# Other pads in SBUF: activations begin, modulo 256 bytes, where the weights begin that they are multiplied with

## The chip, the core and the metric

The kernel is one program on one core of a Trainium2 chip. Its metric is the device time of one execution in microseconds (us). The engines named below are PE (TensorE, matmul), PEld (TensorE's weight loads), DVE (VectorE), ACT (ScalarE), POOL (GpSimd) and SP (SyncE, which issues the DMAs of the weights). SBUF is the on-chip memory from which PE reads both operands of a matmul; a tile's "begin" is its byte address within a partition.

## The reference: what is computed

A trunk of two layers over 256 tokens of width 2048, all in float32. Layer 0 mixes tokens with a Conformer convolution module, layer 1 with multi-head latent attention; each is followed by a squared-ReLU MLP of width 8192. Before every part stands an RMSNorm, after it a residual add, and at the end one more RMSNorm.

```
x = x + conv_module(rms_norm(x), pw1 2048x4096, depthwise width 31, LayerNorm, swish, pw2 2048x2048)
x = x + square(relu(rms_norm(x) @ w1)) @ w2            # w1 2048x8192, w2 8192x2048
x = x + mla(rms_norm(x), w_in 2048x1088, w_q_up 512x3072, w_kv_up 512x4096, w_o 2048x2048)
x = x + square(relu(rms_norm(x) @ w1)) @ w2
out = rms_norm(x)
```

Nearly all arithmetic is in the products with these weights, 364 MB that are read from HBM once.

## The kernel before: stages, tiles and their names

**Products in two parts.** Every float32 operand is written as a high part and a low part in the matmul type float32r (hi, lo for weights; xt, sh and sl, kvh and kvl, qh and ql, oh and ol for activations), and a product is three matmuls: high by high, high by low, low by high. A weight tile comes by DMA into raw; ACT copies it into hi, and DVE (in the convolution also POOL) subtracts to make lo. The profile writes a matmul as `acc<-a,b`: a is the operand that is streamed through the array (256, 288 or 512 columns), b the one that is loaded into it beforehand (128 columns, a PEld row). A weight load runs beside the matmul before it.

**Which operand is streamed.** Three forms matter:

- `mm3` (lines 194 to 196) streams the weights and loads the activations. It carries the second pointwise product of the convolution (pw2, activations sh and sl_, 512 columns), both MLPs' second product (activations sh, sl, gh, gl), the attention's input product (w_in, activations xt, first 288 columns at a time, then 512), its value projections (activations kvh, kvl, 256 columns) and its output product (w_o, activations oh, ol, 512 columns).
- lines 844 to 846 (pw1 of the convolution) stream the activations xt, 256 columns, and load hi and lo. Lines 1408 to 1410 and 1431 to 1433 (keys and queries) do the same with kvh, kvl, qh, ql.
- lines 505 and 506 (both MLPs' first product) load a block of hi and stream 512 columns of xt, high and low part side by side, and then load the block of lo and stream the 256 columns of the high part:

```python
for j in range(8):
    k = 8 * h + j
    nc.tensor.matmul(ps[0], wh[:, j, :], xhl(k), start=k == 0, stop=False)
    nc.tensor.matmul(ps[0][:, :S], wl[:, j, :], xh(k), start=False, stop=k == KC - 1)
```

So one unit of w1, 16 blocks of 128 rows, is 16 pairs of a 512-column and a 256-column matmul. There are 128 such units in the two MLPs, 2048 pairs.

**The order of the work** is written out by hand: inside `tc.manual_schedule()` the instructions of each engine stand in the order of the code. In an MLP, `ORDERS` interleaves the units of w1 (T) with those of w2 that use seven products in place of eight (S) and plain ones (O), so that a unit of 505 and 506 stands between runs of 21 or 24 matmuls of lines 194 to 196. The first 16 units of each MLP follow each other without such runs.

**Where tiles begin.** Tiles are placed by pools, one after the other, each begin a multiple of 32 bytes. Five small tiles that nothing reads are there for the place alone: `pad_const`, `pad_small`, `pad_right` (below xt, and below the attention's keys, values and queries, on the right side of SBUF), `pad_kv` and `pad_o` (in the attention's pool `at`). All of hi, lo and raw begin at 64 modulo 256, in every stage. The blocks that one matmul takes of a tile begin a multiple of 256 bytes further on, except in the first part of w_in (288 columns), where the second half of hi and lo begins 128 further on.

Of the kernel before, what the change touches and what calls it, by code (L numbers as in the profile page):

```python
# [10 lines left out]
F32 = mybir.dt.float32  # L11
# [7 lines left out]
P = 128  # L19
# [16 lines left out]
PARTS = 4  # L36
PAD_CONST = 24
PAD_SMALL = 32
PAD_RIGHT = 48
PAD_KV = 8  # L40
PAD_O = 56
WB = 6
LOOK = WB // 2 - 1
LAST_PE = 22
# [37 lines left out]
def trunk_kernel(  # L82
# [26 lines left out]
    nc = tc.nc  # L109
# [22 lines left out]
    edge = ctx.enter_context(tc.tile_pool(name="edge", bufs=1, side="right"))  # L132
    pad_right = edge.tile([P, PAD_RIGHT], F32, name="pad_right")
    nc.gpsimd.memset(pad_right, 0.0)
# [655 lines left out]
    with ExitStack() as cx:  # L790
        cv = cx.enter_context(tc.tile_pool(name="cv", bufs=1, reuse_waits="tile"))
# [12 lines left out]
        b2 = cv.tile([P, D], F32, name="b2")  # L804

        cn = cv.tile([P, T, D], F32, tag="tok", name="cn")
        sh = cv.tile([P, KC, S], F32R, name="sh")
        sl_ = cv.tile([P, KC, S], F32R, name="sl_")
        stats = cv.tile([P, T, KC // 2, 6], F32, name="stats")

        UC = 2
# [429 lines left out]
    with ExitStack() as cx:  # L1241
        at = cx.enter_context(tc.tile_pool(name="at", bufs=1, reuse_waits="tile"))
# [92 lines left out]
                if h == 1:  # L1335
                    u_load(u + 3)

        pad_kv = at.tile([P, PAD_KV], F32, name="pad_kv")
        nc.gpsimd.memset(pad_kv, 0.0)
        kvh = at.tile([P, KR // P, S], F32R, name="kvh")  # L1340
        kvl = at.tile([P, KR // P, S], F32R, name="kvl")
        qh = at.tile([P, QR // P, S], F32R, name="qh")
# [15 lines left out]
        for i in range(2):  # L1358
            for j in range(HG):
                nc.scalar.activation(qpB[i][DR:, j, :], mq[DR:, :], AF.Copy)  # L1360
        pad_o = at.tile([P, PAD_O], F32, name="pad_o")
        nc.gpsimd.memset(pad_o, 0.0)
# [413 lines left out]
```

## Time and profile before

| | |
|---|---|
| time, median of 3 runs | 1942.49 us (1942.22 to 1942.64) |
| time of the profiled execution | 1942.55 us |
| its span, first to last instruction | 1940.8 us |
| PE busy in the span | 1915.5 us (99%), 10778 matmuls |
| DVE busy | 1652.4 us (85%) |
| ACT busy | 1208.8 us (62%) |
| DMA | 367.62 MB, mean 189 GB/s |
| granted TensorE clock, mean | 0.998 |

PE's rows in the timeline give a start and a length. Matmuls overlap, since the next is started while the last still drains, so a row's length (0.39 us for 512 columns) is more than what the matmul costs. What it costs is the distance from its start to the next one's. Over a run without a stall, first and last start divided by the number of matmuls between them give that price to a fraction of a nanosecond, though single starts are given to 10 ns.

### The profile page before, as it was taken

How to read it: one execution, taken by the hardware profiler on the slowest of the kernel's cores; microseconds unless marked ns; L12 is line 12 of the kernel's file. 1: busy time of each engine (PE TensorE's matmuls, PEld its weight loads, DVE VectorE, ACT ScalarE, POOL GpSimd, SP SyncE). 2: the span in 40 equal slices, each digit the busy share in tenths (PEclk: the TensorE clock that was granted, in tenths of full speed). 3: DMA queues.
4: the chain of work that ended last, by engine and by line, in shares of the span. 5: the costliest groups of instructions: out<-in, count | busy, mean ns of one | idle time of the engine just before them, and what ended most of it. 6: DMA issues, size and time to landing. Idle time of an engine off the chain costs nothing.

```text
span 1940.8 us, 28480 instructions
## 1 busy us (share of the span) xinstructions
PE 1915.5 (99%) x10778; PEld 1673.4 (86%) x10778; DVE 1652.4 (85%) x2372; ACT 1208.8 (62%) x1709; POOL 223.9 (12%) x184
## 2 busy tenths in 40 slices
PE   7999999999999999999999999999999999999998
PEld 7999888888888888888899998888888888888886
DVE  5999865789999999999976665657999999999887
ACT  5556654766666666666566665566766666666654
POOL 5999400000000000000001410000000000000000
PEclk9999999999999999999999999999999999999999
DMA  8666355857666667666646445765667666766663
GB/s 236 184 177 191 133 196 153 227 171 209 200 199 207 197 201 211 197 200 211 202 144 180 118 150 174 206 183 168 200 191 210 208 195 195 214 200 196 210 222 109
DMA packets 407113, 367.62 MB, mean 189 GB/s; under 512 B 15416, under 2 KB 351936, under 8 KB 406720
## 3 DMA queue, kind: packets, MB, share of 16 engines
q1 hardware_dynamic: 405952, 363.63, 62.6%
q10 hardware_dynamic: 1024, 2.17, 0.3%
q8 instruction: 84, 1.38, 0.3%
q14 instruction: 53, 0.43, 0.1%
HBM read 363.68 MB, written 2.10 MB: 188 GB/s over the span
## 4 chain that ended last, share of the span: by engine, by line
PE 95%; DVE 2%; ACT 1%; DMA 1%; POOL 1%; issue 0%; DVEq 0%; ACTq 0%; POOLq 0%
PE acc L505 24%; PE acc L194 15%; PE acc L196 15%; PE acc L195 15%; PE acc L506 12%; PE acc L846 3%; PE acc L845 3%; PE acc L844 3%; PE acc L250 1%; PE sum L894 1%; PE acc L1544 0%; POOL lo L169 0%; DMA xs<-in_x 0%; ACT hi L168 0%; PE acc L1408 0%
## 5 line engine op out<-in xcount | busy, mean ns | idle before, releaser
L505 PE MATMUL acc<-xt,hi 128*128 128x512 f32 x2048 | 716.6, 393 | 0.0
L420 DVE TENSOR_TENSOR lo<-raw,hi 128x1024 fp32r<-128x1024 f32 (+1 forms) x512 | 570.8, 1121 | 92.5 <-ACT hi L419 92.2
L506 PE MATMUL acc<-xt,lo 128*128 128x256 f32 x2048 | 574.2, 280 | 0.5 <-DVE lo L420 0.5
L419 ACT ACTIVATE hi<-raw 128x1024 fp32r<-128x1024 f32 (+1 forms) x512 | 480.3, 971 | 73.2 <-PE acc L195 67.2
L505 PEld LDWEIGHTS acc<-xt,hi 128*128 128x128 f32 x2048 | 384.4, 188 | 87.2
L506 PEld LDWEIGHTS acc<-xt,lo 128*128 128x128 f32 x2048 | 385.2, 188 | 4.1 <-DVE lo L420 0.8
L194 PE MATMUL acc<-hi,sh 128*128 128x512 f32 x930 | 364.3, 392 | 0.0
L196 PE MATMUL acc<-lo,sh 128*128 128x512 f32 x930 | 362.9, 390 | 0.0
L195 PE MATMUL acc<-hi,sl 128*128 128x512 f32 x802 | 312.3, 389 | 0.0
L168 ACT ACTIVATE hi<-raw 128x1024 fp32r<-128x1024 f32 (+2 forms) x184 | 180.0, 1005 | 47.0 <-PE acc L195 41.7
L196 PEld LDWEIGHTS acc<-lo,sh 128*128 128x128 f32 x930 | 174.6, 188 | 37.9
L194 PEld LDWEIGHTS acc<-hi,sh 128*128 128x128 f32 x930 | 174.6, 188 | 36.9
L169 DVE TENSOR_TENSOR lo<-raw,hi 128x1024 fp32r<-128x1024 f32 (+2 forms) x118 | 133.2, 1148 | 68.8 <-ACT hi L168 63.0
L419 ACT ACTIVATE hi<-V 128x1024 fp32r<-128x1024 f32 x94 | 99.6, 1059 | 129.2 <-DVE V L712 118.4
L195 PEld LDWEIGHTS acc<-hi,sl 128*128 128x128 f32 x802 | 150.7, 188 | 28.9
L946 DVE SCALAR_TENSOR_TENSOR sum<-ub,w_dw,sum 128x256 f32<-128x256 f32 x400 | 162.8, 480 | 7.6 <-ACT sum L902 6.5
L169 POOL TENSOR_TENSOR lo<-raw,hi 128x1024 fp32r<-128x1024 f32 x66 | 157.6, 2410 | 24.0 <-ACT hi L168 24.0
L419 ACT ACTIVATE hi<-T 128x1024 fp32r<-128x1024 f32 x94 | 99.4, 1057 | 89.3 <-DVE T L700 80.2
L511 ACT ACTIVATE U<-acc 128x512 f32<-128x512 f32 x128 | 76.2, 595 | 112.5 <-PE acc L506 112.0
L844 PE MATMUL acc<-xt,hi 128*128 128x256 f32 x512 | 145.3, 284 | 0.0
L845 PE MATMUL acc<-xt,hi 128*128 128x256 f32 x512 | 143.9, 281 | 1.0 <-DVE xt L207 1.0
L846 PE MATMUL acc<-xt,lo 128*128 128x256 f32 x512 | 144.0, 281 | 0.1
(270 smaller groups left out, 2797.3 us busy)
## 6 DMA issues: line engine op xcount, KB each, us to landing
raw<-in_mlp_w SPq DMA_DIRECT2D x256, 1024.0 KB, 6.2
raw<-in_conv_w_pw SPq DMA_DIRECT2D x64, 512.0 KB, 5.5
raw<-in_conv_w_pw SPq DMA_DIRECT2D x16, 1024.0 KB, 5.1
raw<-in_mla_w_o SPq DMA_DIRECT2D x16, 1024.0 KB, 5.6
raw<-in_mla_w_kv_up SPq DMA_DIRECT2D x8, 1024.0 KB, 5.5
raw<-in_mla_w_in SPq DMA_DIRECT2D x8, 576.0 KB, 3.8
raw<-in_mla_w_in SPq DMA_DIRECT2D x4, 1024.0 KB, 6.6
raw<-in_mla_w_q_up SPq DMA_DIRECT2D x16, 256.0 KB, 4.6
```

The source lines that it names most:

```text
L168: nc.scalar.activation(hi, raw[:, js, :], AF.Copy)
L169: eng.tensor_tensor(lo, raw[:, js, :], hi.bitcast(F32), op=ALU.subtract)
L194: nc.tensor.matmul(ps, sh, mh, start=start, stop=False)
L195: nc.tensor.matmul(ps, sl, mh, start=False, stop=False)
L196: nc.tensor.matmul(ps, sh, ml, start=False, stop=stop)
L419: nc.scalar.activation(parts[0], src, AF.Copy)
L420: nc.vector.tensor_tensor(parts[1], src, parts[0].bitcast(F32), op=ALU.subtract)
L505: nc.tensor.matmul(ps[0], wh[:, j, :], xhl(k), start=k == 0, stop=False)
L506: nc.tensor.matmul(ps[0][:, :S], wl[:, j, :], xh(k), start=False, stop=k == KC - 1)
L844: nc.tensor.matmul(o, wh[:, bs], xh(k), start=k == 0, stop=False)
L845: nc.tensor.matmul(o, wh[:, bs], xl(k), start=False, stop=False)
L846: nc.tensor.matmul(o, wl[:, bs], xh(k), start=False, stop=k == KC - 1)
```

## The change

Only places change. `pad_right` shrinks from 48 to 40 floats, `pad_kv` goes, `pad_o` grows from 56 to 64 floats, and two new pads stand in the convolution's pool ahead of sh and behind sl_. PE, ACT, DVE and SP run the same instructions in the same order as before, with the same waits; POOL has one instruction less, the memset of `pad_kv`.

```diff
-PAD_RIGHT = 48
-PAD_KV = 8
-PAD_O = 56
+PAD_RIGHT = 40
+PAD_SH = 16
+PAD_STATS = 48
+PAD_O = 64
...
         cn = cv.tile([P, T, D], F32, tag="tok", name="cn")
+        cv.tile([P, PAD_SH], F32, name="pad_sh")
         sh = cv.tile([P, KC, S], F32R, name="sh")
         sl_ = cv.tile([P, KC, S], F32R, name="sl_")
+        cv.tile([P, PAD_STATS], F32, name="pad_stats")
         stats = cv.tile([P, T, KC // 2, 6], F32, name="stats")
...
-        pad_kv = at.tile([P, PAD_KV], F32, name="pad_kv")
-        nc.gpsimd.memset(pad_kv, 0.0)
         kvh = at.tile([P, KR // P, S], F32R, name="kvh")
```

The begins that follow from it, modulo 256 bytes, as the built programs have them:

| tiles | used by | before | after |
|---|---|---|---|
| hi, lo (weights) | all | 64 | 64 |
| xt (turned tokens) | pw1, w1 of both MLPs, w_in | 32 | 64 |
| sh, sl_ (gated rows of the convolution) | pw2 | 0 | 64 |
| kvh, kvl, qh, ql | key, value and query projections | 96 | 64 |
| kpA, kpB, qpB (rotary parts, mask) | scores | 96 | 64 |
| kTh, kTl, qTh, qTl, qpA, vv, pT | scores, values | 32 | 64 |
| sh, sl, gh, gl (hidden rows of the MLPs) | second product of both MLPs | 64 | 64 |
| oh, ol | w_o | 64 | 64 |

Everything else keeps its begin modulo 256 bytes.

## The prediction

> **What bounds the kernel now.** I read the page first: busy time, clock and the chain that ended last.
>
> ```profile
> span 1940.8 us, 28480 instructions
> PE 1915.5 (99%) x10778; PEld 1673.4 (86%) x10778; DVE 1652.4 (85%) x2372; ACT 1208.8 (62%) x1709; POOL 223.9 (12%) x184
> PEclk9999999999999999999999999999999999999999
> PE 95%; DVE 2%; ACT 1%; DMA 1%; POOL 1%; issue 0%; DVEq 0%; ACTq 0%; POOLq 0%
> ```
>
> PE is busy throughout, holds 95% of the chain, and its clock is granted in full. So the time is the sum of what 10778 matmuls cost from start to start, and whatever changes that price changes the time. The page's groups give the counts; their mean ns is a matmul's length and not its price.
>
> ```profile
> L505 PE MATMUL acc<-xt,hi 128*128 128x512 f32 x2048 | 716.6, 393 | 0.0
> L506 PE MATMUL acc<-xt,lo 128*128 128x256 f32 x2048 | 574.2, 280 | 0.5 <-DVE lo L420 0.5
> L844 PE MATMUL acc<-xt,hi 128*128 128x256 f32 x512 | 145.3, 284 | 0.0
> ```
>
> The prices come from PE's timeline: first and last start of a run without a stall, one row each, divided by the matmuls between them. First 512 columns: w_o, then pw2, then the second part of w_in.
>
> ```profile
> 1218.84 0.39 PE L194 MATMUL acc<-hi,oh 128*128 128x512 f32 x1
> ...
> 1237.20 0.39 PE L194 MATMUL acc<-hi,oh 128*128 128x512 f32 x1
> ```
> ```profile
> 280.83 0.39 PE L194 MATMUL acc<-hi,sh 128*128 128x512 f32 x1
> ...
> 298.69 0.39 PE L194 MATMUL acc<-hi,sh 128*128 128x512 f32 x1
> ```
> ```profile
> 1022.59 0.39 PE L194 MATMUL acc<-hi,xt 128*128 128x512 f32 x1
> ...
> 1027.48 0.40 PE L194 MATMUL acc<-hi,xt 128*128 128x512 f32 x1
> ```
>
> The same line, shape and clock, and three prices: 18.36 us for 81 matmuls is 226.7 ns, 17.86 us for 78 is 229.0 ns, 4.89 us for 21 is 232.9 ns. By the table of begins, weights and activations both begin at 64 in w_o; in pw2 the activations begin at 0, in w_in at 32. So the distance of the begins does seem to cost, and 512 columns are cheapest at equal begins. Now 256 columns: pw1 (xt at 32 streamed, weights at 64 loaded), then keys (kvh at 96 streamed), then values (kvh at 96 loaded).
>
> ```profile
> 76.39 0.28 PE L844 MATMUL acc<-xt,hi 128*128 128x256 f32 x1
> ...
> 86.33 0.28 PE L844 MATMUL acc<-xt,hi 128*128 128x256 f32 x1
> ```
> ```profile
> 1045.59 0.28 PE L1408 MATMUL acc<-kvh,hi 128*128 128x256 f32 x1
> ...
> 1048.39 0.28 PE L194 MATMUL acc<-hi,kvh 128*128 128x256 f32 x1
> ...
> 1051.23 0.28 PE L1408 MATMUL acc<-kvh,hi 128*128 128x256 f32 x1
> ```
>
> 9.94 us for 84 is 118.3 ns, 2.80 us for 24 is 116.7 ns, 2.84 us for 24 is 118.3 ns. pw1 and values have one thing in common: the loaded operand begins 32 bytes behind the streamed one. So it is the distance between the two that counts, not either place. Last the pairs of lines 505 and 506, two runs of them:
>
> ```profile
> 348.43 0.39 PE L505 MATMUL acc<-xt,hi 128*128 128x512 f32 x1
> ...
> 392.81 0.39 PE L505 MATMUL acc<-xt,hi 128*128 128x512 f32 x1
> ```
> ```profile
> 1267.62 0.39 PE L505 MATMUL acc<-xt,hi 128*128 128x512 f32 x1
> ...
> 1335.45 0.39 PE L505 MATMUL acc<-xt,hi 128*128 128x512 f32 x1
> ```
>
> 44.38 us for 128 pairs is 346.7 ns; 67.83 us for 192 pairs is 353.3 ns. The instructions and the distance of the begins are the same. So a pair has two rhythms; starting up differently, it stays in one or the other. In the trace 17 of the 128 units run in the dear one (the first two of layer 0's MLP, the first fifteen of layer 1's), 111 in the cheap one. The mean pair is (111 x 346.7 + 17 x 353.3) / 128 = 347.6 ns.
>
> **The change part by part.** No instruction moves on PE, so each term is a count times a difference in price.
>
> *pw2* (384 matmuls, 128 of each line) goes from distance 64 to equal begins: 229.0 to 226.7, -0.9 us. *w_in, second part* (96 matmuls): 232.9 to 226.7, -0.6 us. *w_in, first part* (192 of 288 columns) has half its blocks 128 apart after the change, for which no row stands; I take -0.3 us, between 0 and -0.6 (half of the 6.2 ns that the 512 columns gain, 192 times).
>
> *w_o and the MLPs' second product* are at equal begins already, 0. But they show what equal begins do when the width has just changed. This is a run of w2 behind a unit of w1:
>
> ```profile
> 711.71 0.40 PE L194 MATMUL acc<-hi,sh 128*128 128x512 f32 x1
> ...
> 713.33 0.39 PE L195 MATMUL acc<-hi,sl 128*128 128x512 f32 x1
> 713.56 0.39 PE L196 MATMUL acc<-lo,sh 128*128 128x512 f32 x1
> ...
> 716.28 0.39 PE L196 MATMUL acc<-lo,sh 128*128 128x512 f32 x1
> ```
>
> The first seven take 1.62 us, 231.4 ns each; the last twelve 2.72 us, 226.7 ns. So the 226.7 is not the price of equal begins as such. It is that of a rhythm into which several equal matmuls in a row settle.
>
> *256 columns at equal begins* stand in the scores alone, four in a row behind a stall:
>
> ```profile
> 1080.15 0.27 PE L195 MATMUL acc<-kTh,qTl 128*128 128x256 f32 x1
> ...
> 1080.62 0.28 PE L194 MATMUL acc<-hi,kvh 128*128 128x256 f32 x1
> ```
>
> 0.47 us for four is 117.5 ns, between 116.7 and 118.3. So *pw1* (1536) could gain 1536 x 1.6 ns = 2.5 us if it settles, or lose some 2 us if not; I take 0. *Keys and queries* (384 at 116.7 now) lose at most 0.6 us, *values and the rotary queries* (288 at 118.3) gain at most 0.5; together 0. The scores' own operands move together, 0.
>
> *The pairs* are the large term: 2048 of them, 712 us, and every nanosecond is 2.0 us. No row shows a pair at equal begins. From below: 226.7 for the 512 columns and 116.7 for the 256, 343.4 ns, -8.6 us. From above: the dear rhythm in all units, 353.3 ns, +11.7 us. Between them: the width changes at every matmul of a pair, so the settled 226.7, which took seven of a kind, is not reached; 231.4 and an unsettled 118.3 make 349.7 ns, +4.3 us. What speaks for the upper half is that the same pairs, in a wrong rhythm, do cost 353.3. I take the middle of these two, 351.5 ns: 3.9 x 2048 = +8.0 us.
>
> One rule of the Trainium skill speaks against any effect. TensorE: Matmul & The Clock Gate, section "Step-by-step: what each phase is for", has two independent SBUF read ports on PE, one for the streamed operand and one for the weight load, so that loading the next block takes no bandwidth from the running matmul; by that, pads change nothing. The trace doesn't agree: 226.7, 229.0 and 232.9 ns stand for one instruction.
>
> *The memset of pad_kv*: one on POOL of 105 ns, for which nobody waits.
>
> ```profile
> L1339 POOL MEMSET pad_kv<- x1: 105/105/105, 896.6 to 896.6; 128x8 f32 x1
> ```
>
> Its cover is POOL's idle time (busy 223.9 of 1940.8 us); bare it would be 0.1 us. DVE and ACT read and write the moved tiles 32 or 64 bytes further on, 0 within their slack (85% and 62% busy); if a gain in PE's pace met the wait for DVE's lo, little would be lost, for that wait is 0.5 us in all 2048 of line 506.
>
> *Sum*: 8.0 - 0.9 - 0.6 - 0.3 = +6.2 us on a span of 1940.8; with the 1.75 us around it (1942.55 less 1940.8) that is 1948.8, and the profiled execution is within 0.1 us of the median 1942.49. I forecast 1949, slower.
>
> **The rivals.** *Equal begins suit the pairs too.* Then 512 columns run at 226.7 within a pair and 256 at 116.7: pairs -8.6, pw1 -2.5, pw2 and w_in -1.8, in all -12.9 us, 1929.6. If only the 17 dear units mend, the pairs gain 2048 x 0.9 = 1.8, and with pw1 and the rest it is -6.1, 1936.4; 1933 is the middle. For it: at 512 columns equal is the cheapest of three distances, and a common distance in w1 and w2 might spare the seven dear matmuls at each change. Against it: the cheap rhythm of 346.7 is within 3.3 ns of the two cheapest rows taken together (343.4), so 111 of the 128 units have little left to win and much to lose. It decides if the pair falls under 346 ns.
>
> *Nothing moves beyond the small terms*: pairs and pw1 keep their prices by another rhythm, -1.8 us, 1941; the skill's two ports come to the same, 1942.5 by that rule. Against it: five prices for two shapes in one trace.
>
> *The pads don't do what they say*: excluded as far as places go, the built program has them; only the relation to cost is open.
>
> **How the numbers follow.** Slower by the pairs 0.52, faster by the pairs 0.35, nothing beyond the small terms 0.13. What a measurement here tells from no change is about 0.2%, 3.9 us. The slower case alone reaches from 1945 (+4.3 less 1.8) to 1953 (+11.7 less 1.8), and 1956 if pw1 loses too; the faster one from 1930 to 1937. A tenth at either end left out, the range is 1931 to 1956. Some of the slower case falls inside 0.2%, as does the third: faster 0.35, same 0.14, slower 0.51.
>
> **What would show it.** In the profile after: L505 to L505 at 350 ns or more in most units (right), or under 346 (wrong, the first rival). pw2 and w_in at 226.7 from start to start. pw1 within 116.7 and 119.5. w2's first seven matmuls behind a unit of w1 are where a common rhythm would show. Order, waits and idle time of PE should be as before; a new wait in front of PE would mean that I have the wrong mechanism altogether.

## The result, and the profile after

The changed kernel takes 1951.29 us, median of 4 runs (1950.55 to 1952.12), against 1942.36 us for the kernel before (4 runs, 1942.12 to 1942.64): a ratio of 1.0046, with a 95% interval of 1.0029 to 1.0063. It is slower, by 0.5%. The forecast was 1949. Two runs further down, one of 4960 us of the kernel before and one of 3211 us of the kernel under "All but xt", lie far outside all others of their kernels and are left out of the ratios.

The page of the kernel after, the same rows as were shown of before (the lines of the code stand one to three further down, so 505 is now 506):

```profile
span 1949.9 us, 28480 instructions
PE 1925.8 (99%) x10778; PEld 1679.9 (86%) x10778; DVE 1653.8 (85%) x2372; ACT 1208.9 (62%) x1709; POOL 223.8 (11%) x183
PEclk9999999999999999999999999999999999999999
PE 97%; DVE 1%; ACT 1%; DMA 1%; issue 0%; SPq 0%; DVEq 0%; ACTq 0%
L506 PE MATMUL acc<-xt,hi 128*128 128x512 f32 x2048 | 725.0, 397 | 0.0
L507 PE MATMUL acc<-xt,lo 128*128 128x256 f32 x2048 | 574.9, 281 | 0.6 <-DVE lo L421 0.6
```

POOL has one instruction less, the memset of `pad_kv`; the clock is granted in full, DVE and ACT have what they had, and the wait for lo is 0.6 us in all. PE's busy time grew by 10.3 us, and 8.4 of that is one group: line 506, whose mean length went from 393 to 397 ns. Its 256-column partner, line 507, gained 0.7. PE waits for nothing new; the same matmuls cost more.

Now the prices from PE's timeline. Two stretches of pairs, the first from layer 0, the second from layer 1:

```profile
355.22 0.40 PE L506 MATMUL acc<-xt,hi 128*128 128x512 f32 x1
...
406.10 0.40 PE L506 MATMUL acc<-xt,hi 128*128 128x512 f32 x1
```
```profile
1285.06 0.39 PE L506 MATMUL acc<-xt,hi 128*128 128x512 f32 x1
...
1340.52 0.39 PE L506 MATMUL acc<-xt,hi 128*128 128x512 f32 x1
```

50.88 us for 144 pairs is 353.3 ns; 55.46 us for 160 pairs is 346.6 ns. These are the two means that the kernel before had, at the same two places, exchanged: before, layer 0's stretch was the cheap one and layer 1's the dear one. Over the trace 109 of the 128 units run dear once settled and 17 cheap: the second and third unit of layer 0's MLP, the second to sixteenth of layer 1's. Before, just these 17 were the dear ones and 109 the cheap. (The prediction took the first two and the first fifteen for the dear ones and all others for cheap. The first unit of each MLP, which is entered from the transposes of xt, is in neither count here; its later pairs were dear before, 353.3 and 352.3 ns, and are cheap after.)

The cheap rhythm is the same pair again and again. The dear one is not, and it has another form after the change: before, pairs of 345.7 and 360.9 ns took turns; after, two pairs of 349.6 in the mean are followed by one of 360.8. Both come to 353.3. The expectations further down give the dear price as 353.5 or 353.6 and mean the same rhythm.

Then the smaller terms: pw1, keys, pw2 and the second part of w_in.

```profile
76.74 0.28 PE L847 MATMUL acc<-xt,hi 128*128 128x256 f32 x1
...
86.46 0.28 PE L847 MATMUL acc<-xt,hi 128*128 128x256 f32 x1
```
```profile
1057.32 0.28 PE L1409 MATMUL acc<-kvh,hi 128*128 128x256 f32 x1
...
1060.08 0.28 PE L1411 MATMUL acc<-kvh,lo 128*128 128x256 f32 x1
```
```profile
281.31 0.39 PE L195 MATMUL acc<-hi,sh 128*128 128x512 f32 x1
...
298.99 0.39 PE L195 MATMUL acc<-hi,sh 128*128 128x512 f32 x1
```
```profile
1029.01 0.39 PE L195 MATMUL acc<-hi,xt 128*128 128x512 f32 x1
...
1033.79 0.39 PE L195 MATMUL acc<-hi,xt 128*128 128x512 f32 x1
```

pw1: 9.72 us for 81 matmuls, 120.0 ns where it was 118.3. Keys: 2.76 us for 23, 120.0 where it was 116.7. So 256 columns at equal begins cost 120 ns, the dearest of the three. pw2: 17.68 us for 78, 226.7 where it was 229.0. w_in: 4.78 us for 21, 227.6 where it was 232.9. So 512 columns at equal begins, one after the other, are the cheapest.

Last, a run of w2 behind a unit of w1:

```profile
432.60 0.40 PE L195 MATMUL acc<-hi,sh 128*128 128x512 f32 x1
...
433.99 0.39 PE L195 MATMUL acc<-hi,sh 128*128 128x512 f32 x1
...
437.16 0.39 PE L197 MATMUL acc<-lo,sh 128*128 128x512 f32 x1
```

The first six cost 231.7 ns each (1.39 us), the other fourteen 226.4 (3.17 us). In the mean of the 74 such runs the first six cost 230.8 ns, where they cost 231.8 before. It still has to settle at each handover, though xt now begins where sh and the weights begin.

The ledger, made from all the starts of both timelines (each matmul's start to the next one's, with the stalls in it):

| part | before to after, us |
|---|---|
| the pairs of w1 (mean 348.4 to 352.4 ns; 347.8 to 351.8 without the five pairs that hold a stall) | +8.2 |
| pw1 | +1.5 |
| keys and queries | +0.5 |
| values and the rotary part of the queries | +0.4 |
| transposes, stalls included | +0.6 |
| w2 of both MLPs | -0.9 |
| pw2 | -0.6 |
| w_in, both parts | -0.6 |
| sum, and the span's change | +9.1 |

From here on a mean pair leaves out the five that hold a stall, and a mean of pw1 the 21 or 22 of its 1536 matmuls that do.

### The profile page after: what moved, and what is told of

Its sections match the earlier page's. It is cut to its first block, busy times and chain, and to the rows that moved or that the text cites. A ratio compares the mean times of both kernels' runs of the same rounds, so it can differ in the third digit from the quotient of the medians.

```text
span 1949.9 us, 28480 instructions
## 1 busy us (share of the span) xinstructions
PE 1925.8 (99%) x10778; PEld 1679.9 (86%) x10778; DVE 1653.8 (85%) x2372; ACT 1208.9 (62%) x1709; POOL 223.8 (11%) x183
## 4 chain that ended last, share of the span: by engine, by line
PE 97%; DVE 1%; ACT 1%; DMA 1%; issue 0%; SPq 0%; DVEq 0%; ACTq 0%
PE acc L506 24%; PE acc L195 15%; PE acc L196 15%; PE acc L197 15%; PE acc L507 12%; PE acc L848 3%; PE acc L847 3%; PE acc L849 3%; PE acc L251 1%; PE sum L897 1%; DMA xs<-in_x 0%; PE acc L1432 0%; PE acc L1433 0%; PE acc L1434 0%; PE acc L1409 0%; PE acc L1410 0%
## 5 line engine op out<-in xcount | busy, mean ns | idle before, releaser
L506 PE MATMUL acc<-xt,hi 128*128 128x512 f32 x2048 | 725.0, 397 | 0.0
```

## Experiments

The theory to test: the price of a matmul depends on how far apart, modulo 256 bytes, its two operands begin, the pairs of w1 carry the change, and equal begins are bad for them because the width changes at every matmul. The rivals: the place in SBUF itself counts and not the distance; the small parts carry it; the rhythm is set only by how a unit is entered.

**Only xt moves.** The kernel before with one pad changed.

```diff
-PAD_RIGHT = 48
+PAD_RIGHT = 40
```

> Only xt (and the attention's keys, queries and values) move from 32 to 64; the gated rows, the latents and the rotary parts stay as before. If the pairs of lines 505 and 506 carry the change, this alone gives 1942.4 + 8.2 (pairs) + 1.5 (pw1) - 0.6 (w_in) = 1951.5 us, and pairs cost 353.6 ns in some 110 of 128 units. If the loss came from the other moved tiles, it stays at 1942 to 1944.

Measured: 1951.8 us (4 runs, 1950.23 to 1953.28) against 1940.87 for the kernel before on the same chip, a ratio of 1.0054 (1.0039 to 1.0069). From its page, and a unit of pairs between two runs of w2 from PE's timeline:

```profile
span 1948.4 us, 28480 instructions
L505 PE MATMUL acc<-xt,hi 128*128 128x512 f32 x2048 | 723.9, 397 | 0.0
```
```profile
710.53 0.39 PE L505 MATMUL acc<-xt,hi 128*128 128x512 f32 x1
...
715.82 0.40 PE L505 MATMUL acc<-xt,hi 128*128 128x512 f32 x1
```

15 pairs in 5.29 us, 352.7 ns. Here 98 units are dear and 28 cheap, the mean pair is 351.3 ns, and pw1 is at 120.0. One pad smaller by 32 bytes makes the whole loss, within the interval.

**All but xt.** The changed kernel with that pad put back.

```diff
-PAD_RIGHT = 40
+PAD_RIGHT = 48
```

> The whole change without the move of xt: gated rows and latents at 64, xt at 32. By the matmuls' prices: pw2 -0.5 us, keys, queries and values +0.9 us, pairs 0: 1942.8 us, within 0.1% of before, with pairs at 346.7 ns in 111 units. If moving the rest matters on its own, it is more than 2 us away from before.

Measured: 1942.49 us (median of 10 runs), a ratio of 1.0006 (0.9996 to 1.0016): not to be told from no change.

```profile
L506 PE MATMUL acc<-xt,hi 128*128 128x512 f32 x2048 | 716.0, 393 | 0.0
```
```profile
706.75 0.40 PE L506 MATMUL acc<-xt,hi 128*128 128x512 f32 x1
...
711.95 0.39 PE L506 MATMUL acc<-xt,hi 128*128 128x512 f32 x1
```

15 pairs in 5.20 us, 346.7 ns, 113 units cheap and 13 dear. The 13 are not among those that were dear in the kernel before: here the fourth to sixteenth unit of layer 0's MLP are dear, and all of layer 1's are cheap, though xt and the weights begin where they did. By the same ledger pw2 gained 0.6 us, keys and queries lost 0.5 and values 0.4: the small parts nearly cancel. The two ratios together, 1.0060, agree with the 1.0046 of the whole change within their intervals.

**The weights move, not xt.** The kernel before, xt where it was (32), and all tiles of the weights' side of SBUF moved to 32 modulo 256.

```diff
-PAD_CONST = 24
+PAD_CONST = 16
```

> The other way round: xt stays at 32, and the weights with everything on the left side of SBUF move from 64 to 32, so that xt and weights begin together without xt being moved. If the distance of the two begins sets the price, the pairs cost 353.6 ns in most units, pw1 120 ns, and the time is 1951 us as after the change. If it is xt's place at 64 as such, the pairs stay at 346.7 and the time at 1942.

Measured in one run: 1951.82 us.

```profile
span 1950.0 us, 28480 instructions
```
```profile
712.10 0.39 PE L505 MATMUL acc<-xt,hi 128*128 128x512 f32 x1
...
717.39 0.40 PE L505 MATMUL acc<-xt,hi 128*128 128x512 f32 x1
```

352.7 ns a pair, 111 units dear, pw1 at 120.0: the changed kernel's prices, with xt where the faster kernel has it. For equal begins it is the distance between the two that counts and not either place.

**Another way into a unit.** The changed kernel with a 128-column transpose ahead of each unit of w1. It adds 128 matmuls of its own.

```diff
                             ps.append(acc_tile())
+                            nc.tensor.transpose(ps[0][:, :P], ident, ident)
```

> The changed kernel with one 128-column transpose more ahead of each of the 128 units of w1 (its result is overwritten). It adds some 128 x 110 to 170 ns = 14 to 22 us of its own. If the rhythm of a unit is set by how it is entered, the transpose ends the hand-over from w2's run, and the units behind w2 no longer stand at 353.6: all 128 units come out in one rhythm, most likely 346.7 ns a pair. If equal begins as such make the pairs dear, the units behind w2 stay at 353.6 and only the first fifteen of layer 1 are at 346.7.

Measured in one run: 1965.6 us. The 14.3 us over the changed kernel are the transposes and what they hold up, 112 ns for each of the 128. A unit from PE's timeline, with its transpose:

```profile
714.85 0.27 PE L503 MATMUL acc<-ident 128*128 128x128 f32 x1
714.88 0.48 PE L507 MATMUL acc<-xt,hi 128*128 128x512 f32 x1
...
715.32 0.40 PE L507 MATMUL acc<-xt,hi 128*128 128x512 f32 x1
...
720.26 0.40 PE L507 MATMUL acc<-xt,hi 128*128 128x512 f32 x1
```

From the second pair on, 14 pairs take 4.94 us, 352.9 ns. 104 units are dear and 22 cheap. That is a miss: breaking the handover from w2 doesn't bring the cheap rhythm. Not nothing, though: within the first sixteen units of an MLP, which had been in one rhythm for thirteen units or more, two dear and two cheap ones now mostly take turns. So a disturbance at the entry does change a unit's rhythm, but which one it falls into isn't decided by coming from w2 alone.

**Grouped by width.** The changed kernel, with the sixteen matmuls of a chunk in another order: eight of 512 columns, and then the eight of 256.

```diff
                             nc.tensor.matmul(ps[0], wh[:, j, :], xhl(k), start=k == 0, stop=False)
+                        for j in range(8):
+                            k = 8 * h + j
                             nc.tensor.matmul(ps[0][:, :S], wl[:, j, :], xh(k), start=False, stop=k == KC - 1)
```

> The changed kernel (equal begins) with the 16 matmuls of a chunk of w1 in another order: first the eight of 512 columns, then the eight of 256, instead of pairs. Same matmuls, same operands. If equal begins are dear in the pairs because the width changes at every matmul, a 512 now costs between 226.7 ns (settled) and 231.4 (the seven behind a change of width), a 256 120 ns as in pw1: 346.7 to 351.4 ns for two, 1938 to 1948 us. If equal begins are dear for xt in any order, two stay at 353.5 ns and the time at 1951.

Measured in one run: 1943.36 us, against 1942.18 in one of the kernel before beside it. In PE's timeline eight matmuls make one row here:

```profile
628.72 1.98 PE L506 MATMUL acc<-xt,hi 128*128 128x512 f32 x8
630.53 1.11 PE L509 MATMUL acc<-xt,lo 128*128 128x256 f32 x8
631.49 2.00 PE L506 MATMUL acc<-xt,hi 128*128 128x512 f32 x8
633.33 1.12 PE L509 MATMUL acc<-xt,lo 128*128 128x256 f32 x8
634.28 0.40 PE L195 MATMUL acc<-hi,sh 128*128 128x512 f32 x1
```

Sixteen pairs in 5.56 us are 347.5 ns in this unit, 348.0 in the mean over all: 229.0 for the 512 columns and 119.1 for the 256. The begins are equal as in the changed kernel, and of its 8.9 us 1.2 are left; by the ledger the pairs take 8.6 us less than there. So the pairs' loss at equal begins goes away when the widths are grouped. Alternating widths need not bring it, though: 17 units of the changed kernel alternate at equal begins and cost 346.7, less than the grouped ones. (Grouping also parts the blocks of hi from those of lo. That this alternation costs nothing is likely, since pw2 runs hi, hi, lo at 226.7, but it wasn't tried alone, nor was grouping at the begins of before.)

**Other distances.** The kernel before with other values of `PAD_RIGHT`, one run each, beside one run of the kernel before (1943.91 for begins 0, 96, 128 and 192; 1942.18 for 160 and 224). Single runs of the kernel before lie anywhere from 1940.5 to 1944.5 us, so the prices in the traces say more here than the times do. The pad also moves the scores' operands, which by the ledger changes 0.1 us at most.

> The kernel before with xt at 0 instead of 32, so that the weights (64) begin 64 behind xt in pw1 and the pairs. If the change's loss is that of equal begins alone, the pairs fall back to 346.7 ns in most units and the time to 1941 to 1944. If any distance but 32 lets most units fall into the dear rhythm, pairs stand at 353 and the time at 1950.

> xt at 96, 32 behind the weights: the distance at which keys and queries (256 columns streamed) stood at 116.7 ns before the change. pw1 should come to 116.7 ns, 1536 x 1.6 ns = -2.5 us; for the pairs no row of this distance exists. With pairs as before 1938 to 1940; with pairs in the dear rhythm 1948 to 1950.

> xt at 128, 64 behind the weights. By 512 columns at a distance of 64 (pw2 before, 229.0 ns) a small loss against equal begins there; for the pairs the map is open: 1941 if most units keep the cheap rhythm of 346.7 ns, 1950 if most take the dear one of 353.5.

> The kernel before with xt at 160. Between xt at 128 (pairs 349.9 ns in the mean, pw1 117.7) and 192 (350.6 and 118.5), if the price changes steadily with the distance: pairs 350, pw1 118, 1945 us. If each distance falls into a rhythm of its own, it can lie anywhere from 347 to 354 ns.

> xt at 192, half of 256 away from the weights. If prices repeat every 256 bytes and depend on the distance, this is the farthest from equal begins, and pw1 and the pairs are no dearer than before: 1938 to 1943. If they repeat every 128 bytes, it is the same as equal begins: pairs at 353.5, pw1 at 120, 1951.

> The kernel before with xt at 224. Between xt at 192 (pairs 350.6 ns) and at 0 (353.2; pw1 114.4 and thereby the cheapest), if the price changes steadily: pairs 352, pw1 116, 1949 us. If each distance has a rhythm of its own, anywhere from 347 to 354 ns.

| xt begins at (weights at 64) | PAD_RIGHT | us | mean pair, ns | pw1, ns | what 126 units do once settled |
|---|---|---|---|---|---|
| 0 | 56 | 1952.61 | 353.2 | 114.7 | 353.3 in all |
| 32 (before) | 48 | 1943.91, 1942.18 | 347.8 | 118.4 | 109 cheap, 17 dear |
| 64 (only xt) | 40 | 1951.8 | 351.3 | 120.0 | 28 cheap, 98 dear |
| 96 | 96 | 1938.27 | 347.5 | 116.7 | 346.7 in all |
| 128 | 88 | 1944.49 | 349.8 | 117.8 | 348.8 in 109, 353.3 in 17 |
| 160 | 80 | 1950.06 | 350.4 | 119.9 | 350.0 in all |
| 192 | 72 | 1947.79 | 350.4 | 118.7 | 351 in all |
| 224 | 64 | 1938.34 | 347.1 | 118.3 | 346.7 in all |

(The prices at 32 are those of the first trace of the kernel before.)

The prices follow no line in the distance: 0 and 64, one either side of the begin that the kernel before had, are the dearest, 96 and 224 the cheapest. Nor do they repeat every 128 bytes, for 192 doesn't give what 64 gives. At 96, with the weights 32 below the streamed xt, pw1 has the 116.7 ns that keys had at that distance before the change. And one distance suits one shape and not another: begin 0 is the worst for the pairs and the best for pw1, which there has two rhythms of its own, from PE's timeline of that kernel on either side of two transposes:

```profile
99.93 0.28 PE L844 MATMUL acc<-xt,hi 128*128 128x256 f32 x1
...
106.73 0.28 PE L844 MATMUL acc<-xt,hi 128*128 128x256 f32 x1
...
108.00 0.28 PE L844 MATMUL acc<-xt,hi 128*128 128x256 f32 x1
...
117.89 0.28 PE L844 MATMUL acc<-xt,hi 128*128 128x256 f32 x1
```

6.80 us for 60 matmuls is 113.3 ns, 9.89 for 84 is 117.7: the same line, operands and distance, before and behind them. And the time at begin 0 holds something else than prices. From the rows of PE's waits and of a stretch:

```profile
PE sum L894 <- DVE ub L869: 4.3, 1, 4.3
204.20:211.00 6.80, 5.54 (x13) 4.47 (x14) 6.80 (x20) 3.60 (x6) 5.35 (x5) 0.50 0.01 2
```

At 3.7 ns less for each of 1536 matmuls pw1 should give 5.7 us; by the ledger it gives 2.4, since PE comes earlier to its last convolution products (line 894) and waits there for DVE, 4.3 us where it was 1.1 before. From 204.2 to 211.0 us the granted clock is 0.50 (before, it is 1.00 in the same stage), and most of the first twelve of those products cost 426 ns in place of 216: 2.7 us more by the ledger. So nothing of pw1's gain is left.

**The best of it together.** The kernel before with xt at 224, and the convolution's two pads from the change, which put sh and sl_ at 64; kvh, kvl, qh and ql stay at 96.

```diff
-PAD_RIGHT = 48
+PAD_RIGHT = 64
+PAD_SH = 16
+PAD_STATS = 48
...
```

> What the map recommends, against the kernel before: xt at 224, the gated rows of the convolution at 64, keys' and queries' latents left at 96. If the terms add up: 1942.4 - 4.1 (xt at 224: pairs in the cheap rhythm in all units, and shorter settling in w2) - 0.5 (pw2 at equal begins) = 1937.8 us, 0.24% faster than before. If the gain of the single look at xt 224 was scatter between runs, it is within 0.1% of before.

Measured in 10 runs: 1937.70 us (1937.53 to 1937.93), 0.9973 of the kernel before (0.9963 to 0.9982). It beats both kernels. A handover and a run of w2 from PE's timeline:

```profile
710.12 0.39 PE L507 MATMUL acc<-xt,hi 128*128 128x512 f32 x1
...
710.47 0.39 PE L196 MATMUL acc<-hi,sh 128*128 128x512 f32 x1
...
711.83 0.39 PE L196 MATMUL acc<-hi,sh 128*128 128x512 f32 x1
```

The first six matmuls of w2 cost 226.7 ns here (1.36 us) and 227.2 in the mean of the 74 runs, against 230.8 in the changed kernel and 231.8 in the one before: there is hardly anything to settle. By the ledger against the kernel before, w2 gives -2.8 us, the pairs -1.2, pw2 -0.6 and w_in -0.3, and the span is 4.8 us shorter. So the larger part comes from w2, whose own operands were not moved.

## Why the prediction was right, point by point

*What bounds it*, and that the price from start to start is the thing to read: right. No large wait came or went: pw1's price alone would give +2.4 us, and 1.0 less of stalls leaves the ledger's +1.5. The direction, though, stood at a chance of 0.51, and the range, 1931 to 1956, holds the first rival's middle as well; that the time lies in it says little.

*The pairs*, +8.0 forecast, +8.2 measured. The size came out by another way than the working had it. The forecast took 351.5 ns as a price of its own, midway between a composed 349.7 and the dear rhythm of 353.3. No unit settles at 351.5: 109 settle in the dear rhythm, the upper bound, and 17 in the cheap one. The mean, 347.8 before and 351.8 after, is lower than the dear rhythm for two reasons, by the starts in the trace. In the 84 units behind a run of w2 the first five pairs cost 350.0 ns in the mean (the very first 340.0, where it was 351.6 before) and only the eleven behind them 353.6, so that these units go from 347.0 to 352.5. And in the 42 that follow another unit of w1 directly, the exchange of the 17 leaves a mean of 350.5 before and 351.9 after, stalls included. So +5.5 ns in 1344 pairs and +1.4 in 672, less 0.1 us in the two first units, make the 8.2 us. The sign and the bounds were argued; that the middle between them met the mean was luck.

*Why equal begins are bad for the pairs*: that the width changes at each matmul, so that the price into which equal ones settle isn't reached. The grouped kernel bears that out in part, 348.0 against 351.8 with the same begins. It doesn't say why 17 units alternate at equal begins in the cheap rhythm. The same experiment shows that the forecast put the loss too evenly: in the changed kernel 235 ns of the pair are the 512 columns and 117 the 256, against 230 and 118 before. All of it is in the 512.

*pw1* was taken as 0, in a range of -2.5 to +2; it was +1.5. This step was mis-sized. It leaned on four matmuls of the scores at 117.5 ns, too few and behind a stall, and the settled price at equal begins is 120.0, outside the 116.7 to 119.5 that were given as the sign. *Keys, queries and values* were to come out at 0 together; they lost 0.9, since the same 120 ns took the place of 116.7 and 118.3 alike, and the gain that values were to bring against it was a loss.

*pw2 and w_in* were to be at 226.7 from start to start: 226.7 and 227.6. Their terms, 1.8 us in all, came to 1.2, because part of each stage is stalls and settling, which a settled price doesn't count. *w2* was taken as 0 and gained 0.9 by shorter settling, which the rows of the first seven matmuls could have hinted at. These errors, +1.5, +0.9, +0.6 for transposes, +0.6, -0.9 and 0.2 from the pairs, add up to the 2.9 us between the forecast sum of +6.2 and the measured +9.1.

*The rivals.* That equal begins suit the pairs too is excluded by the 109 dear units; that nothing moves beyond the small terms, by the kernel in which xt alone moves. The rule of two independent read ports, from the Trainium skill (TensorE: Matmul & The Clock Gate, section "Step-by-step: what each phase is for"), leaves no room for the distance, as the prediction reads it; the kernel with only the weights moved and the one with only xt moved contradict that reading, by more than 10 us each. The traces don't show the two reads themselves.

*What stays open*: what in the chip makes a rhythm, and what picks one of two for a unit. Shown are that the distance of the two begins decides which prices exist, that at equal begins grouping the widths takes the pairs' loss away, and that the first sixteen units of an MLP can fall otherwise than those behind w2. A transpose at the entry changed some units and not most, so the handover alone isn't it. Which rhythm the first units take may well differ from one execution to the next: the runs of the kernel before lie near 1940.8, 1942.2 and 1944 us, and by an estimate from the rhythms thirteen units that change theirs are 13 x 16 x 6.6 ns = 1.4 us, sixteen are 1.7. With xt at 224, where all units have one rhythm, the ten runs of the last kernel lie within 0.4 us. Only one execution of each kernel was traced, so this isn't shown.

## What to carry to other kernels

Where PE is busy from end to end, read its price from start to start, by line and by stage, before looking for waits: a matmul has several prices at the same shape and clock, and the placement of its two operands, modulo 256 bytes, is one of the things that pick them. No simple rule (equal, or one half apart) gave the best place here, so try the eight distances for the stage that has the most matmuls, and look at the shapes one by one, since the best distance for 256 columns can be the worst for 512 and 256 in turn. If widths alternate, try grouping them too. And look at what a faster stage runs into: at begin 0 pw1's gain went into a longer wait and a lower granted clock behind it.

## What the runs showed of the hardware that was not expected

- Two rhythms for the same instructions and the same distance: 346.7 and 353.3 ns a pair at both 32 and 0 apart, in exchanged places of the program; 113.3 and 117.7 ns for pw1 at 64 apart, on either side of two transposes. The 353.3 has a period of two pairs at 32 apart (345.7, 360.9) and of three at 0 (349.6 twice, 360.8).
- 256 columns streamed against weights with equal begins cost 120.0 ns, the most of the distances tried (119.9 with xt at 160), while 512 columns at equal begins settle at 226.7, the least.
- How a unit of w1 ran changes the price of the w2 products behind it, though no operand of w2 had moved: in the mean their first six cost 227.2 ns with xt at 224, 230.8 with xt at 64, and 228.4 with xt at 64 and a transpose ahead of the unit.
